# Softmax sums as two float32r parts, formed one step later, in a two-branch attention layer

## The chip, the cores and the metric

The kernel runs on one core of one Trainium2 chip. The metric is the device time of one execution in microseconds, the median of several executions. Engines are named as in the profile: PE (TensorE), DVE (VectorE), ACT (ScalarE), POOL (GpSimd), SP (SyncE, which issues the DMAs here).

## The reference

One encoder layer over 2048 prompt tokens and 512 sample tokens, all in float32. The stage around the change is softmax attention in two branches of 8 heads each (grouped-query, then latent):

```python
s = jnp.einsum('bqgrd,bkgd->bgrqk', qblk, k, preferred_element_type=jnp.float32) * scale
p = jax.nn.softmax(s, axis=-1).astype(v.dtype)
return jnp.einsum('bgrqk,bkgd->bqgrd', p, v)
```

Ahead of it stand the modulated RMS norm, the input projections, norms and rotations of queries and keys; behind it the gated output projections. Neither is touched.

## The kernel before

A number that float32r cannot hold is kept as a high part (its float32r rounding) and a low part (the rest), and products are made from the parts.

**Jobs and steps.** `attention` works through 80 jobs (`specs`): branch, head, and query chunk c of 512 queries. Chunks 0 to 3 are long jobs (2048 keys, 16 key tiles, 8 pairs), chunk 4 is a short one (512 keys, 2 pairs). Keys lie on partitions. One step of the main loop handles one pair n of key tiles; there are 34 steps a head. The order on each engine is the order in which the loop emits (manual schedule).

**One step.** `scores` writes the pair's scores into one of two `st` banks of PSUM (L980: 2 matmuls a key tile in the first branch, 3 in the second). ACT exponentiates the bank twice: rounded to float32r into `ph` (L983, six buffers, the high part), and in place in float32 (L984). `lows` has DVE subtract the two into `pl` (L993, four buffers, the low part), which also frees the bank. Two steps later (`BACK`; three for a job's first pair) `values` multiplies both parts with the values: `pv` (X, one bank, L1003) and `py` (Y, one bank, L1004); at most three key tiles in a step. Between them `advance` issues the maximum stream of a job some 12 steps ahead: two matmuls into the single `mp` bank (L947), reduced by DVE (L950). Since a first pair waits three steps, a step with no value matmuls follows each long job; the prediction calls it the hole. It is the step of pair 2 of the next job.

**Sums.** The softmax sum of a query is row 64 of Y. The low parts bring theirs in through columns of ones in `vt`. For the high parts of a long job, POOL adds the pairs n < `direct` = 7 into `acc` (L986), folds its two halves (L988), and PE adds the fold through the selector `sel` in one float32 matmul (L1008) behind the last key tile. The last pair goes straight in through a float32r selector (L1006). Short jobs use the selector for all their tiles.

**Job end.** `finish` copies X and Y out on ACT (L1015, L1016); POOL adds Y to the lower half of X (L1027) and, three steps later, the two halves (L1029); SP stores sums and output.

Of the kernel before, what the change touches and what calls it, by code (L numbers as in the profile page):

```python
# [9 lines left out]
F32 = mybir.dt.float32  # L10
F32R = mybir.dt.float32r
AF = mybir.ActivationFunctionType
ALU = mybir.AluOpType
# [4 lines left out]
P = 128  # L18
# [5 lines left out]
CH = 512  # L24
# [119 lines left out]
VW = 130  # L144
# [614 lines left out]
def attention(tc, nc, env, h4):  # L759
    e = NS(env)  # L760
    dma, nm, f32 = e.dma, e.nm, e.f32
    ha, fl, filler, cur, rest = h4
    kp = Pool(tc, "kp", "left")
# [25 lines left out]

    zero_q(kp)  # L790
    zero_q(kp)
    sel = [kp.tile([P, VW - 64], t, name=f"sel{n}") for n, t in enumerate((F32, F32R))]
    for a in (sel[0], f32(sel[1])):
        nc.vector.memset(a, 0.0)
        nc.vector.memset(a[:, 64:VW - 64], 1.0)
    tops = [[kp.tile([P, 32], F32, name=f"m{s}{n}") for s in "pt"] for n in range(3)]
    for m, _ in tops:
        nc.vector.memset(m, 0.0)
# [44 lines left out]
    def start(i, br, h, c):  # L843

        j = Job()
        j.br, j.h, j.c = br, h, c
        j.last = (br, h, c) == specs[-1]
        smp = int(c == 4)
        j.nk = (NS_TOK if smp else NP_TOK) // P
        j.direct = 0 if smp else j.nk // 2 - 1  # L850
        j.k1, j.k2, j.vt = kcur[(*kv_of(br, h), smp)]
        j.k3 = k3s[smp]
        qn, qr = q_src(br, h, c)
        j.qz = qzs[i % 3]
        j.qm = kp.tile([P, CH], F32R, tag="qm", name=nm("qm"), bufs=4)
        if br == 0:
            dma(f32(j.qm), qn[0].partition_broadcast(2))
            j.km = j.k1
            j.scale = SC_A
        else:  # L860
            dma(f32(j.qm[0:64, :]), qn[0])
            dma(f32(j.qm[64:128, :]), qr[0].partition_broadcast(2))
            j.km = j.k2
            j.scale = SC_B
        j.mx = kp.tile([P, 4, 2], F32, tag="mx", name=nm("mx"), bufs=3)
        return j
# [15 lines left out]
    at = Pool(tc, "at", "left")  # L882
# [35 lines left out]
    jobs = []  # L918
# [7 lines left out]
    def due(last=False):  # L926
        while queue and (last or queue[0][0] <= clock[0]):
            queue.pop(0)[2]()
# [37 lines left out]
            later(1, row)  # L966
            yield True

    def scores(j, n):

        if n == 0:
            if j.direct:
                j.acc = at.tile([P, 2, CH], F32, tag="acc", name=nm("acc"), bufs=2)
            j.hs, j.ls = [], []
        st = pp.tile([P, 2, CH], F32, tag="st", name=nm("st"), bufs=2)
        for a in range(2):
            kt = 2 * n + a
            ps = j.passes(j, slice(kt * P, (kt + 1) * P))
            for i, (k, q) in enumerate(ps):
                nc.tensor.matmul(st[:, a, :], lhsT=k, rhs=q, start=(i == 0), stop=(i == len(ps) - 1))  # L980
        h = at.tile([P, 2, CH], F32R, tag="ph", name=nm("ph"), bufs=6)
        j.hs.append(h)
        nc.scalar.activation(out=h, in_=st, func=AF.Exp, scale=j.scale)  # L983
        nc.scalar.activation(out=st, in_=st, func=AF.Exp, scale=j.scale)  # L984
        if 0 < n < j.direct:
            nc.gpsimd.tensor_tensor(out=j.acc, in0=f32(j.hs[0]) if n == 1 else j.acc, in1=f32(h), op=ALU.add)  # L986
            if n == j.direct - 1:
                nc.gpsimd.tensor_tensor(out=j.acc[:, 0, :], in0=j.acc[:, 0, :], in1=j.acc[:, 1, :], op=ALU.add)  # L988
        return st

    def lows(j, st):
        l = at.tile([P, 2, CH], F32R, tag="pl", name=nm("pl"), bufs=4)
        nc.vector.tensor_tensor(out=l, in0=st, in1=f32(j.hs[-1]), op=ALU.subtract)  # L993
        j.ls.append(l)

    def values(j, kt):

        if kt == 0:
            j.X, j.Y = x_bank(), y_bank()
        n, a = kt // 2, kt % 2  # L1000
        y = j.Y[0:VW - 64, :]
        st, sp = kt == 0, kt == j.nk - 1
        nc.tensor.matmul(j.X, lhsT=j.vt[:, kt, 0:P], rhs=j.hs[n][:, a, :], start=st, stop=sp)  # L1003
        nc.tensor.matmul(y, lhsT=j.vt[:, kt, 64:VW], rhs=j.ls[n][:, a, :], start=st, stop=False)  # L1004
        if n >= j.direct:
            nc.tensor.matmul(y, lhsT=sel[1], rhs=j.hs[n][:, a, :], start=False, stop=sp and not j.direct)  # L1006
        if sp and j.direct:
            nc.tensor.matmul(y, lhsT=sel[0], rhs=j.acc[:, 0, :], start=False, stop=True)  # L1008
        return j if sp else None

    def finish(j):

        y = at.tile([VW - 64, CH], F32, tag="y", name=nm("ys"), bufs=2)
        xa = at.tile([P, CH], F32, tag="xa", name=nm("xa"), bufs=2)
        nc.scalar.copy(out=xa, in_=j.X)  # L1015
        nc.scalar.copy(out=y, in_=j.Y[0:VW - 64, :])  # L1016
        later(1, lambda: dma(e.sums[j.br][j.c, j.h:j.h + 1, :], y[64:65, :]))
        if j.h == 7 and not j.last:
            for k, step in enumerate(inverse(nc, e, at, j.br, j.c)):
                later(6 + 2 * k, step)  # L1020
        if (j.br, j.h, j.c) == (1, 7, 0):
            for k, step in enumerate(tail_load(nc, e, wt, 1, 0, first_y)):
                later(13 + 3 * k, step)

        def rest():
            s = at.tile([64, CH], F32, tag="s", name=nm("s"), bufs=2)
            nc.gpsimd.tensor_tensor(out=xa[0:64, :], in0=xa[0:64, :], in1=y[0:64, :], op=ALU.add)  # L1027
            later(1, lambda: dma(s, xa[64:128, :]))
            later(3, lambda: nc.gpsimd.tensor_tensor(out=s, in0=s, in1=xa[0:64, :], op=ALU.add))  # L1029
            later(5, lambda: dma(  # L1030
                e.o_s[j.br][j.h // 2, 64 * (j.h % 2):64 * (j.h % 2) + 64, j.c * CH:(j.c + 1) * CH], s))

        return rest
# [4 lines left out]
    def advance(to):  # L1038
        while done[0] < to and next(stream, None) is not None:
            done[0] += 1  # L1040
# [5 lines left out]
    with contextlib.ExitStack() as order:  # L1046
# [14 lines left out]
        passes = {0: start_main(0, *specs[0])}  # L1061
        order.close()
        order.enter_context(tc.manual_schedule(engines={eng.PE, eng.Activation, eng.DVE, eng.Pool, eng.SP}))
        ready, g = [], -1
        while g + 1 < len(steps) or ready:
            g += 1
            clock[0] = g
            st, rest = None, None
            if g < len(steps):
                i, n = steps[g]  # L1070
                br, h, c = specs[i]
                if c < 2 and n == 4:
                    late = [0]

                    def post_later(out, in_):
                        later(late[0], lambda: post_now(out, in_))
                        late[0] += 1

                    if c == 0 and i + 5 < len(specs):
                        load_k(*kv_of(*specs[i + 5][0:2]), 0, post_later)  # L1080
                    if c == 1:
                        load_k(*kv_of(br, h), 1, post_later)
                if n == 0:
                    for k in range(i + 1, min(i + 3, len(specs))):
                        if k not in passes and (k == i + 1 or pairs[i + 1] < 8):
                            passes[k] = start_main(k, *specs[k])
                    jobs[i].passes = passes.pop(i)
                    if specs[i] == (1, 0, 0):
                        for k in range(4):
                            later(24 * k + 4, lambda k=k: wa.append(load_raw(nc, e, wt, e.a_out, k)))  # L1090
                            later(24 * k + 12, lambda k=k: wa.append(
                                split_raw(nc, e, wt, "wa", wa.pop(), k, nc.gpsimd)))
                        for m, step in enumerate(tail_load(nc, e, wt, 0, 0, first_y)):
                            later(24 * m + 100, step)
                        later(180, lambda: y0.extend(split_y(nc, e, wt, 0, first_y.pop())))
                st = scores(jobs[i], n)
                ready += [(g + BACK + (n == 0), jobs[i], 2 * n + a) for a in range(2)]
            now = sum(r[0] <= g for r in ready)
            for m in range(min(now, 3)):
                if m == 1:  # L1100
                    advance(lead + g + 1)
                _, j, kt = ready.pop(0)
                if values(j, kt):
                    rest = finish(j)
            if now < 2:
                advance(lead + g + 1)
            due()
            if st is not None:
                lows(jobs[i], st)
            if rest:  # L1110
                rest()
# [217 lines left out]
```

## Time and profile before

| | |
|---|---|
| median of 3 runs | 3220.47 us (3214.39 to 3221.25) |
| profiled execution | 3216.27 us, span 3214.5 us |
| granted TensorE clock | 0.994 of full speed (2.4 GHz) |
| busy share of the span | PE 98%, DVE 60%, POOL 57%, ACT 51% |
| attention, first branch | about 1233 to 1928 us |
| attention, second branch | about 1928 to 2746 us |

How to read it: a matmul record begins when its rows start to flow and ends some way into the next one's, so records overlap, and a busy PE says little by itself. The distance of two starts tells what a matmul costs. A record that is longer than its like, or starts later, has been held.

### The profile page before, as it was taken

The numbers are of one execution on the slowest core, as the hardware profiler recorded it, in microseconds if no ns is written. First come the engines' busy times: TensorE is split into PE (matmuls) and PEld (weight loads), VectorE is DVE, ScalarE is ACT, GpSimd is POOL, SyncE is SP. The second block draws the span as 40 slices with busy tenths as digits, with TensorE's granted clock in tenths as the row PEclk, the third lists the DMA queues.
The fourth block names the chain that finished last, engine by engine and source line by source line (L and its number), as shares of the span: only waits on it lengthen the run. The fifth ranks groups of instructions, "written<-read, shape, count | busy, mean of one in ns | idle before, by whom it ended". The sixth has DMA issues, their size and how long they took to land.

```text
span 3214.5 us, 41877 instructions
## 1 busy us (share of the span) xinstructions
PE 3146.4 (98%) x15214; PEld 2538.8 (79%) x15214; DVE 1919.8 (60%) x2441; ACT 1635.3 (51%) x2169; POOL 1820.4 (57%) x1124
## 2 busy tenths in 40 slices
PE   7999999999999989999999999999999999899999
PEld 6988889988889877777777777777777777799997
DVE  5733214532205227999999998887887887544443
ACT  5332234232224226888888877777676777321122
POOL 6422123421224336888888887777776778644443
PEclk9999999999999999999999999999999999999999
DMA  8445542365634741112111134433433222665552
GB/s 244 146 150 204 189 159 90 120 201 180 205 103 151 223 144 55 40 37 68 42 48 36 38 88 105 99 91 84 94 93 86 67 66 69 197 190 164 162 175 73
DMA packets 283922, 383.89 MB, mean 119 GB/s; under 512 B 31916, under 2 KB 185844, under 8 KB 281252
## 3 DMA queue, kind: packets, MB, share of 16 engines
q1 hardware_dynamic: 283716, 381.22, 40.1%
q8 instruction: 120, 1.97, 0.3%
q14 instruction: 86, 0.70, 0.1%
HBM read 251.52 MB, written 118.96 MB: 115 GB/s over the span
## 4 chain that ended last, share of the span: by engine, by line
PE 87%; DMA 4%; DVE 3%; issue 2%; ACT 2%; POOL 1%; SPq 1%; ACTq 0%; POOLq 0%; DVEq 0%
PE st L980 18%; PE mm L604 17%; PE mm L340 8%; PE mp L947 8%; PE py L1004 7%; PE pv L1003 7%; PE z L1270 6%; PE ab L1204 6%; PE mm L692 3%; PE py L1008 2%; PE py L1006 1%; SPq L44 1%; PE pv L604 1%; DMA raw<-in_w_in 1%; PE py L604 1%
## 5 line engine op out<-in xcount | busy, mean ns | idle before, releaser
L986 POOL TENSOR_TENSOR acc<-acc,ph 128x1024 f32<-128x1024 f32 x320 | 768.8, 2403 | 56.1 <-ACT ph L983 42.0
L950 DVE TENSOR_REDUCE mx<-mp 128x1 f32<-128x1024 f32 x512 | 625.9, 1222 | 218.1 <-PE mp L947 217.1
L983 ACT ACTIVATE ph<-st 128x1024 fp32r<-128x1024 f32 x544 | 558.5, 1027 | 364.7 <-PE st L980 357.0
L993 DVE TENSOR_TENSOR pl<-st,ph 128x1024 fp32r<-128x1024 f32 x544 | 658.2, 1210 | 37.9 <-ACT st L984 37.5
L984 ACT ACTIVATE st<-st 128x1024 f32<-128x1024 f32 x544 | 555.5, 1021 | 0.0
L209 POOL TENSOR_TENSOR wl<-wraw,wh 128x1536 fp32r<-128x1536 f32 (+3 forms) x59 | 189.0, 3214 | 508.8 <-ACT wh L208 508.2
L980 PE MATMUL st<-qm,k 128*128 128x512 f32 x1024 | 434.1, 424 | 9.1 <-DVE pl L993 8.4
L980 PE MATMUL st<-qz,k 128*128 128x512 f32 x1056 | 416.1, 394 | 0.0
L1003 PE MATMUL pv<-ph,vt 128*128 128x512 f32 x1024 | 404.3, 395 | 4.0 <-ACT xa L1015 3.6
L1004 PE MATMUL py<-pl,vt 128*66 128x512 f32 x1024 | 404.7, 395 | 0.0
L947 PE MATMUL mp<-k,qm 128*128 128x512 f32 x1024 | 323.4, 397 | 0.4 <-DVE mx L950 0.4
L604 PE MATMUL mm<-hh,wh 128*128 128x512 f32 x768 | 302.2, 394 | 0.0
L604 PE MATMUL mm<-hl,wh 128*128 128x512 f32 x768 | 301.8, 393 | 0.0
L604 PE MATMUL mm<-hh,wl 128*128 128x512 f32 x768 | 301.8, 393 | 0.0
L980 PEld LDWEIGHTS st<-qm,k 128*128 128x128 f32 x1024 | 192.2, 188 | 110.2 <-DVE pl L993 35.8
L947 PEld LDWEIGHTS mp<-k,qm 128*128 128x128 f32 x1024 | 190.6, 188 | 73.4 <-DVE mx L950 11.9
L986 POOL TENSOR_TENSOR acc<-ph,ph 128x1024 f32<-128x1024 f32 x64 | 153.0, 2390 | 161.7 <-ACT ph L983 161.7
L1003 PEld LDWEIGHTS pv<-ph,vt 128*128 128x128 f32 x1024 | 192.6, 188 | 61.8 <-ACT xa L1015 10.6
L980 PEld LDWEIGHTS st<-qz,k 128*128 128x128 f32 x1056 | 198.5, 188 | 47.6 <-issue 7.4
L340 PE MATMUL mm<-wh,hh 128*128 128x384 f32 (+1 forms) x640 | 210.9, 330 | 5.1 <-ACT hh L60 2.7
L340 PE MATMUL mm<-wl,hh 128*128 128x384 f32 (+1 forms) x640 | 210.1, 329 | 0.0
L340 PE MATMUL mm<-wh,hl 128*128 128x384 f32 (+1 forms) x640 | 205.8, 330 | 0.0
(235 smaller groups left out, 5782.5 us busy)
## 6 DMA issues: line engine op xcount, KB each, us to landing
wraw<-in_w_in SPq DMA_DIRECT2D x46, 768.0 KB
x<-in_x_prompt SPq DMA_DIRECT2D x32, 512.0 KB
wada<-in_ada_w SPq DMA_DIRECT2D x24, 512.0 KB
raw<-in_w_in SPq DMA_DIRECT2D x48, 256.0 KB
vb<-uv SPq DMA_DIRECT2D x20, 512.0 KB
qm<-aqh SPq DMA_DIRECT2D x40, 256.0 KB
s<-xa SPq DMA_DIRECT2D x80, 128.0 KB
mt<-ma SPq DMA_DIRECT2D x40, 256.0 KB
```

The costliest lines, as they stand in the source:

```text
L340: nc.tensor.matmul(ps[:, 0:n], lhsT=lt, rhs=rt, start=(i == 0), stop=(i == 23))
L604: nc.tensor.matmul(ps, lhsT=lt, rhs=rt[:, k, :], start=(i == 0), stop=(i == 23))
L947: nc.tensor.matmul(mp[:, a, :], lhsT=j.qm[:, qt * P:(qt + 1) * P], rhs=j.km[:, kc * CH:(kc + 1) * CH], start=True, stop=True)
L950: nc.vector.tensor_reduce(out=j.mx[:, n // 2, n % 2:n % 2 + 1], in_=mp.rearrange("p a k -> p (a k)"), axis=AX.X, op=ALU.max)
L980: nc.tensor.matmul(st[:, a, :], lhsT=k, rhs=q, start=(i == 0), stop=(i == len(ps) - 1))
L983: nc.scalar.activation(out=h, in_=st, func=AF.Exp, scale=j.scale)
L984: nc.scalar.activation(out=st, in_=st, func=AF.Exp, scale=j.scale)
L986: nc.gpsimd.tensor_tensor(out=j.acc, in0=f32(j.hs[0]) if n == 1 else j.acc, in1=f32(h), op=ALU.add)
L993: nc.vector.tensor_tensor(out=l, in0=st, in1=f32(j.hs[-1]), op=ALU.subtract)
L1003: nc.tensor.matmul(j.X, lhsT=j.vt[:, kt, 0:P], rhs=j.hs[n][:, a, :], start=st, stop=sp)
L1004: nc.tensor.matmul(y, lhsT=j.vt[:, kt, 64:VW], rhs=j.ls[n][:, a, :], start=st, stop=False)
L1204: nc.tensor.matmul(ps[:, dd, :], lhsT=a, rhs=b, start=(i == 0), stop=(i == 11))
```

## The change

The float32 sum matmul goes. ACT rounds the fold to float32r and POOL subtracts to get its low part (`sum_parts`, one `ph` buffer for both); this is emitted in the next job's first step, between the two exps. Two float32r matmuls (`sums`) add the parts to Y one step after the job's last key tile, which is the hole. The X copy stays where it was (`finish`); the Y copy and all that follows it move one step back (`finish_sums`). In the first branch `direct` is 6: one pair fewer in POOL's sum, two more selector matmuls. There too, the last pair's full exp goes to SBUF (a `pl` buffer) and its low part is subtracted by POOL and not by DVE (`low_by_pool`). Short jobs are as before.

```diff
--- before.py
+++ after.py
@@ -789,10 +789,9 @@
 
     zero_q(kp)
     zero_q(kp)
-    sel = [kp.tile([P, VW - 64], t, name=f"sel{n}") for n, t in enumerate((F32, F32R))]
-    for a in (sel[0], f32(sel[1])):
-        nc.vector.memset(a, 0.0)
-        nc.vector.memset(a[:, 64:VW - 64], 1.0)
+    sel = kp.tile([P, VW - 64], F32R, name="sel")
+    nc.vector.memset(f32(sel), 0.0)
+    nc.vector.memset(f32(sel[:, 64:VW - 64]), 1.0)
     tops = [[kp.tile([P, 32], F32, name=f"m{s}{n}") for s in "pt"] for n in range(3)]
     for m, _ in tops:
         nc.vector.memset(m, 0.0)
@@ -847,7 +846,8 @@
         j.last = (br, h, c) == specs[-1]
         smp = int(c == 4)
         j.nk = (NS_TOK if smp else NP_TOK) // P
-        j.direct = 0 if smp else j.nk // 2 - 1
+        j.parts = not smp
+        j.direct = 0 if smp else j.nk // 2 - 2 + br
         j.k1, j.k2, j.vt = kcur[(*kv_of(br, h), smp)]
         j.k3 = k3s[smp]
         qn, qr = q_src(br, h, c)
@@ -966,7 +966,7 @@
             later(1, row)
             yield True
 
-    def scores(j, n):
+    def scores(j, n, ended):
 
         if n == 0:
             if j.direct:
@@ -981,6 +981,12 @@
         h = at.tile([P, 2, CH], F32R, tag="ph", name=nm("ph"), bufs=6)
         j.hs.append(h)
         nc.scalar.activation(out=h, in_=st, func=AF.Exp, scale=j.scale)
+        if ended:
+            sum_parts(ended)
+        if low_by_pool(j, n):
+            full = at.tile([P, 2, CH], F32, tag="pl", name=nm("pf"), bufs=4)
+            nc.scalar.activation(out=full, in_=st, func=AF.Exp, scale=j.scale)
+            return full
         nc.scalar.activation(out=st, in_=st, func=AF.Exp, scale=j.scale)
         if 0 < n < j.direct:
             nc.gpsimd.tensor_tensor(out=j.acc, in0=f32(j.hs[0]) if n == 1 else j.acc, in1=f32(h), op=ALU.add)
@@ -988,7 +994,22 @@
                 nc.gpsimd.tensor_tensor(out=j.acc[:, 0, :], in0=j.acc[:, 0, :], in1=j.acc[:, 1, :], op=ALU.add)
         return st
 
+    def sum_parts(j):
+
+        a = j.acc[:, 0, :]
+        j.sum = at.tile([P, 2, CH], F32R, tag="ph", name=nm("hl"), bufs=6)
+        nc.scalar.copy(out=j.sum[:, 0, :], in_=a)
+        nc.gpsimd.tensor_tensor(out=j.sum[:, 1, :], in0=a, in1=f32(j.sum[:, 0, :]), op=ALU.subtract)
+
+    def low_by_pool(j, n):
+        return j.br == 0 and j.parts and n == j.nk // 2 - 1
+
     def lows(j, st):
+        if low_by_pool(j, len(j.ls)):
+            l = at.tile([P, 2, CH], F32R, tag="pl", name=nm("pl"), bufs=4)
+            nc.gpsimd.tensor_tensor(out=l, in0=st, in1=f32(j.hs[-1]), op=ALU.subtract)
+            j.ls.append(l)
+            return
         l = at.tile([P, 2, CH], F32R, tag="pl", name=nm("pl"), bufs=4)
         nc.vector.tensor_tensor(out=l, in0=st, in1=f32(j.hs[-1]), op=ALU.subtract)
         j.ls.append(l)
@@ -1003,16 +1024,22 @@
         nc.tensor.matmul(j.X, lhsT=j.vt[:, kt, 0:P], rhs=j.hs[n][:, a, :], start=st, stop=sp)
         nc.tensor.matmul(y, lhsT=j.vt[:, kt, 64:VW], rhs=j.ls[n][:, a, :], start=st, stop=False)
         if n >= j.direct:
-            nc.tensor.matmul(y, lhsT=sel[1], rhs=j.hs[n][:, a, :], start=False, stop=sp and not j.direct)
-        if sp and j.direct:
-            nc.tensor.matmul(y, lhsT=sel[0], rhs=j.acc[:, 0, :], start=False, stop=True)
+            nc.tensor.matmul(y, lhsT=sel, rhs=j.hs[n][:, a, :], start=False, stop=sp and not j.direct)
         return j if sp else None
 
+    def sums(j):
+        for k in range(2):
+            nc.tensor.matmul(j.Y[0:VW - 64, :], lhsT=sel, rhs=j.sum[:, k, :], start=False, stop=k == 1)
+
     def finish(j):
 
+        j.xa = at.tile([P, CH], F32, tag="xa", name=nm("xa"), bufs=2)
+        nc.scalar.copy(out=j.xa, in_=j.X)
+
+    def finish_sums(j):
+
+        xa = j.xa
         y = at.tile([VW - 64, CH], F32, tag="y", name=nm("ys"), bufs=2)
-        xa = at.tile([P, CH], F32, tag="xa", name=nm("xa"), bufs=2)
-        nc.scalar.copy(out=xa, in_=j.X)
         nc.scalar.copy(out=y, in_=j.Y[0:VW - 64, :])
         later(1, lambda: dma(e.sums[j.br][j.c, j.h:j.h + 1, :], y[64:65, :]))
         if j.h == 7 and not j.last:
@@ -1061,8 +1088,8 @@
         passes = {0: start_main(0, *specs[0])}
         order.close()
         order.enter_context(tc.manual_schedule(engines={eng.PE, eng.Activation, eng.DVE, eng.Pool, eng.SP}))
-        ready, g = [], -1
-        while g + 1 < len(steps) or ready:
+        ready, ending, g = [], [], -1
+        while g + 1 < len(steps) or ready or ending:
             g += 1
             clock[0] = g
             st, rest = None, None
@@ -1093,7 +1120,7 @@
                         for m, step in enumerate(tail_load(nc, e, wt, 0, 0, first_y)):
                             later(24 * m + 100, step)
                         later(180, lambda: y0.extend(split_y(nc, e, wt, 0, first_y.pop())))
-                st = scores(jobs[i], n)
+                st = scores(jobs[i], n, jobs[i - 1] if i and n == 0 and jobs[i - 1].parts else None)
                 ready += [(g + BACK + (n == 0), jobs[i], 2 * n + a) for a in range(2)]
             now = sum(r[0] <= g for r in ready)
             for m in range(min(now, 3)):
@@ -1101,9 +1128,17 @@
                     advance(lead + g + 1)
                 _, j, kt = ready.pop(0)
                 if values(j, kt):
-                    rest = finish(j)
+                    finish(j)
+                    if j.parts:
+                        ending.append((g + 1, j))
+                    else:
+                        rest = finish_sums(j)
             if now < 2:
                 advance(lead + g + 1)
+            if ending and ending[0][0] == g:
+                j = ending.pop(0)[1]
+                sums(j)
+                rest = finish_sums(j)
             due()
             if st is not None:
                 lows(jobs[i], st)
```

PE at the end of a first-branch long job and after. Ahead of these rows stands the last key tile's `pv`. Before:

```order
L1004 MATMUL py_10908<-pl_11012,vt_9397 66x512
L1006 MATMUL py_10908<-ph_10997,sel_9418 66x512
L1008 MATMUL py_10908<-acc_10834,sel_9417 66x512
L980 MATMUL st_11062<-qm_10636,k_9395 128x512
L980 MATMUL st_11062<-qz_10194,k_9396 128x512
L980 MATMUL st_11062<-qm_10636,k_9395 128x512
L980 MATMUL st_11062<-qz_10194,k_9396 128x512
L947 MATMUL mp_11074<-k_9395,qm_10822 128x512 x2
```

Now, from the hole's maximum matmuls to the next job's first matmul into Y (`py_11099`; `hl` holds the sum's two parts):

```order
L947 MATMUL mp_11077<-k_9395,qm_10819 128x512 x2
L1032 MATMUL py_10909<-hl_11026,sel 66x512 x2
L980 MATMUL st_11089<-qm_10633,k_9395 128x512
L980 MATMUL st_11089<-qz_10191,k_9396 128x512
L980 MATMUL st_11089<-qm_10633,k_9395 128x512
L980 MATMUL st_11089<-qz_10191,k_9396 128x512
L1024 MATMUL pv_11098<-ph_11024,vt_9397 128x512
L1025 MATMUL py_11099<-pl_11040,vt_9397 66x512
```

The sum's matmul stood ahead of the hole's four score matmuls; its two parts now stand behind them, with the next step's four score matmuls and one value matmul between them and the first one that writes the next job's Y.

ACT at the same place, from the first exp of the next job's pair 0 on. Before:

```order
L983 ACTIVATE ph_11021<-st_11016 128x1024
L984 ACTIVATE st_11016<-st_11016 128x1024
L983 ACTIVATE ph_11039<-st_11034 128x1024
L984 ACTIVATE st_11034<-st_11034 128x1024
L1015 COPY xa_11055<-pv_10907 128x512
L1016 COPY ys_11054<-py_10908 66x512
L983 ACTIVATE ph_11067<-st_11062 128x1024
L984 ACTIVATE st_11062<-st_11062 128x1024
L983 ACTIVATE ph_11087<-st_11082 128x1024
```

Now:

```order
L983 ACTIVATE ph_11024<-st_11019 128x1024
L1001 CAST hl_11026<-acc_10831 128x512
L990 ACTIVATE st_11019<-st_11019 128x1024
L983 ACTIVATE ph_11047<-st_11042 128x1024
L990 ACTIVATE st_11042<-st_11042 128x1024
L1037 COPY xa_11061<-pv_10908 128x512
L983 ACTIVATE ph_11070<-st_11065 128x1024
L990 ACTIVATE st_11065<-st_11065 128x1024
L1043 COPY ys_11083<-py_10909 66x512
L983 ACTIVATE ph_11094<-st_11089 128x1024
L990 ACTIVATE st_11089<-st_11089 128x1024
```

The copy of Y (`ys`) stood ahead of the hole's two exps, right behind that of X, and stands behind them now; between the two exps of pair 0 stands the rounding of the sum (`CAST hl`).

POOL in the first branch, from the job's last additions to the next job's first. Before:

```order
L1029 TENSOR_TENSOR s_10879<-s_10879,xa_10874 64x512
L986 TENSOR_TENSOR acc_10834<-acc_10834,ph_10955 128x1024
L986 TENSOR_TENSOR acc_10834<-acc_10834,ph_10975 128x1024
L988 TENSOR_TENSOR acc_10834<-acc_10834 128x512
L986 TENSOR_TENSOR acc_11015<-ph_11021,ph_11039 128x1024
```

Now:

```order
L992 TENSOR_TENSOR acc_10831<-acc_10831,ph_10931 128x1024
L992 TENSOR_TENSOR acc_10831<-acc_10831,ph_10957 128x1024
L994 TENSOR_TENSOR acc_10831<-acc_10831 128x512
L1056 TENSOR_TENSOR s_10897<-s_10897,xa_10874 64x512
L1010 TENSOR_TENSOR pl_11015<-pf_11000,ph_10998 128x1024
L1002 TENSOR_TENSOR hl_11026<-acc_10831,hl_11026 128x512
L992 TENSOR_TENSOR acc_11018<-ph_11024,ph_11047 128x1024
L992 TENSOR_TENSOR acc_11018<-acc_11018,ph_11070 128x1024
```

One addition is gone; the addition of the previous job's halves (`s`) moved behind the fold, and the last pair's low part (`pl`) and the sum's low part (`hl`) stand between it and the next job's first addition.

## Rows read from the trace of the kernel before

**Rows 1.** Windows of the two branches: busy us (instructions) by engine, then clock, DMA.

```profile
1233.00:1928.00 695.00, 688.39 (x2850) 492.05 (x2849) 640.39 (x615) 560.83 (x616) 592.65 (x299) 1.00 0.19 49
1928.00:2746.00 818.00, 810.24 (x3413) 603.74 (x3412) 646.31 (x613) 573.30 (x634) 621.08 (x313) 1.00 0.35 85
```

**Rows 2.** Timeline, PE, end of a first-branch job: start, us, engine, line, tiles.

```profile
1709.14 1.02 PE L1008 MATMUL py<-acc,sel 128*66 128x512 f32 x2
...
1710.24 0.39 PE L980 MATMUL st<-qz,k 128*128 128x512 f32 x1
...
1712.56 0.39 PE L1004 MATMUL py<-pl,vt 128*66 128x512 f32 x1
1712.87 0.74 PE L947 MATMUL mp<-k,qm 128*128 128x512 f32 x2
1713.44 0.39 PE L1003 MATMUL pv<-ph,vt 128*128 128x512 f32 x1
...
1714.13 0.40 PE L1004 MATMUL py<-pl,vt 128*66 128x512 f32 x1
1714.44 0.50 PE L980 MATMUL st<-qm,k 128*128 128x512 f32 x1
1714.78 0.39 PE L980 MATMUL st<-qz,k 128*128 128x512 f32 x1
```

**Rows 3.** Timeline, PE: f32 sums one head later, and a head apart.

```profile
1796.71 1.02 PE L1008 MATMUL py<-acc,sel 128*66 128x512 f32 x2
...
2082.35 1.02 PE L1008 MATMUL py<-acc,sel 128*66 128x512 f32 x2
...
2183.57 1.02 PE L1008 MATMUL py<-acc,sel 128*66 128x512 f32 x2
```

**Rows 4.** Timeline, PE, first branch: first and last held maximum matmul of 23.

```profile
1253.70 0.73 PE L947 MATMUL mp<-k,qm 128*128 128x512 f32 x2
...
1910.23 0.73 PE L947 MATMUL mp<-k,qm 128*128 128x512 f32 x2
```

**Rows 5.** Timeline, PE, behind a short job: last score matmul, first value matmuls.

```profile
1758.61 0.40 PE L980 MATMUL st<-qz,k 128*128 128x512 f32 x1
1759.51 0.50 PE L1003 MATMUL pv<-ph,vt 128*128 128x512 f32 x1 [0.51 <-ACT xa L1015]
...
1760.27 0.62 PE L947 MATMUL mp<-k,qm 128*128 128x512 f32 x2
```

**Rows 6.** Timeline, ACT, same place: last exp, copies of X and Y.

```profile
1757.93 1.02 ACT L984 ACTIVATE st<-st 128x1024 f32<-128x1024 f32 x1
1758.88 0.59 ACT L1015 COPY xa<-pv 128x512 f32<-128x512 f32 x1
1759.35 0.58 ACT L1016 COPY ys<-py 66x512 f32<-66x512 f32 x1
```

**Rows 7.** Timeline, ACT, the two exps of the hole of rows 2.

```profile
1711.19 1.02 ACT L983 ACTIVATE ph<-st 128x1024 fp32r<-128x1024 f32 x1 [0.41 <-PE st L980]
1712.11 1.02 ACT L984 ACTIVATE st<-st 128x1024 f32<-128x1024 f32 x1
```

**Rows 8.** Timeline, ACT, second branch: first exp of a hole.

```profile
2186.05 1.03 ACT L983 ACTIVATE ph<-st 128x1024 fp32r<-128x1024 f32 x1 [0.85 <-PE st L980]
```

**Rows 9.** Groups of instructions by line: count, busy us, mean ns, idle before.

```profile
L986 POOL TENSOR_TENSOR acc<-acc,ph 128x1024 f32<-128x1024 f32 x320 | 768.8, 2403 | 56.1 <-ACT ph L983 42.0 <-DMA s<-xa 0.5 <-DMA qz<-mt 0.2
...
L993 DVE TENSOR_TENSOR pl<-st,ph 128x1024 fp32r<-128x1024 f32 x544 | 658.2, 1210 | 37.9 <-ACT st L984 37.5
...
L984 ACT ACTIVATE st<-st 128x1024 f32<-128x1024 f32 x544 | 555.5, 1021 | 0.0
...
L988 POOL TENSOR_TENSOR acc<-acc 128x512 f32<-128x512 f32 x64 | 82.7, 1292 | 5.0
...
L258 POOL TENSOR_TENSOR ada<-wada,ada 128x1024 fp32r<-128x1024 f32 x8 | 27.5, 3446 | 7.4 <-ACT ada L256 7.4
...
L1147 POOL TENSOR_TENSOR wal<-raw,wah 128x1024 fp32r<-128x1024 f32 x4 | 9.6, 2402 | 3.8 <-ACT wah L1146 3.8
```

## The prediction

> **What bounds the kernel now.** I read the windows of the two branches first [rows 1]: the granted clock is 1.00 and PE is busy 688 of 695 us in the first branch and 810 of 818 us in the second. That busy figure is not yet proof, because matmul records overlap, so I then counted issue slots in the timeline. Ten 512-column matmuls issue between 1710.24 and 1712.56 us [rows 2], 0.232 us each; I use 0.231 us as one slot. A head of five jobs takes 1796.71 - 1709.14 = 87.6 us in the first branch and 2183.57 - 2082.35 = 101.2 us in the second [rows 2, 3]. Its slots: in the first branch a long job issues 32 score, 32 value, 16 maximum and 2 selector matmuls, 82 slots, and one f32 sum; the short job issues 24. The f32 sum starts at 1709.14; the second score matmul behind it starts at 1710.24, so the first began at 1710.01, and the sum held PE for 0.87 us [rows 2]. Together 352 x 0.231 + 4 x 0.87 = 84.8 us of 87.6. The second branch has two more score matmuls for each key tile: 420 x 0.231 + 4 x 0.87 = 100.5 of 101.2. So PE's order sets the end in both branches, and what counts is slots and PE's waits, 2.8 us a head in the first branch and 0.7 in the second.
>
> Where the 2.8 us lie: after the hole (the step in which no value matmuls are due) PE is held four times, 1712.87 - 1712.56 - 0.23 = 0.08, then 0.11, 0.08 and 0.11 us, 0.38 us together [rows 2]. The same piece stands 23 times in the branch, the first at 1253.70 and the last at 1910.23 [rows 4]. Those are waits for DVE (the single maximum bank, the score banks). Once a head, behind the short job, the next job's first value matmuls wait for ACT's copies of X and Y: 1759.51 - 1758.61 - 0.23 = 0.67 us and then 1760.27 - 1759.51 - 0.46 = 0.30, 0.97 in all [rows 5]. The rest, 2.8 - 0.97 - 3 x 0.38 = 0.7 us a head, is scattered.
>
> **The price of a copy just ahead of its reader.** Rows 5 and 6 give it for this kernel: the Y copy starts 0.95 + 0.47 us after the exp before it; the matmul into Y issues at 1760.27 - 0.23 = 1760.04, so 0.69 us after its copy's start at 1759.35. The copies themselves start 0.95 us after the start of the exp ahead of them (1758.88 - 1757.93).
>
> **Slots.** The f32 sum (0.87 us) becomes two slots (0.46). In the second branch that is all: -0.41 us x 32 long jobs = -13.1 us. In the first, two more selector matmuls are added: 4 x 0.231 - 0.87 = +0.05, x 32 = +1.7 us.
>
> **The Y copy, one step later.** It used to follow the X copy ahead of the hole; now the sum is formed in the hole and Y is copied behind the hole's two exps, while the next step's second value matmul already wants the single Y bank. First branch, T being the hole's first score matmul: the first exp starts at T + 1.18 (1710.01 to 1711.19), the second 0.92 later, the copy 0.95 after that, T + 3.05, and Y is free for PE at T + 3.05 + 0.69 = 3.74 [rows 2, 5, 6, 7]. PE gets there after 8 slots of the hole and 5 of the next step, 13 x 0.231 = 3.00. A wait of 0.74 us in each long job, 32 x 0.74 = +23.7 us. Second branch: the exp starts 1.61 us after the hole's first score matmul (2183.57 + 0.87 = 2184.44 to 2186.05 [rows 3, 8]), Y is free at 1.61 + 0.92 + 0.95 + 0.69 = 4.17, PE arrives after 17 slots at 3.93: 0.24 x 32 = +7.7 us. Ends: 0 and these values, if something else already holds PE there; I take the full values, as the chain starts from PE's own score matmuls and slides with them.
>
> **Waits that go.** The 0.38 us behind the hole are waits for DVE at the matmuls right behind the held one; PE now arrives there 0.74 us later, and DVE has one subtraction less a job (1.21 us [rows 9]). I let all 23 go: -8.7 us. The short job's 0.97 us stays (its end is not changed), and the scattered 0.7 us a head stays, with 0 as its other end.
>
> **The low part on GpSimd.** Its duration is not there for this pair of tiles. Nearest: the additions of the same size in the same stage, 2.40 us, and the same subtraction at the weights, 2.40; far end: the same subtraction at the modulation, 3.45 [rows 9]. I take 2.40, the stage's own row. With T7 the last pair's first score matmul, the full exp ends near T7 + 1.18 + 0.92 + 1.02 = 3.1 and the low part at 5.5; its matmul stands 27 slots behind T7, at 6.24. So 0.7 us of cover if GpSimd is free, and its work of a long job, 6 x 2.40 + 4 x 1.29 = 19.6 us, fits into the job's 20.8. Cost taken as 0; if that cover is gone, each microsecond more is PE's.
>
> In the 3.45 us row VectorE ran the other half of the same subtraction, both inputs in SBUF. The Trainium skill (SBUF — State Buffer, section "SBUF: two separate sides") says that such a VectorE instruction and a GpSimd instruction shut each other out of a shared port pair for whole instructions. By that rule the 2.40 stands here, since VectorE's subtraction in attention reads one input from PSUM; the trace agrees, 320 additions beside it with a mean of 2403 ns [rows 9].
>
> **Hidden parts.** ACT's copy of the sum's high part delays the second exp of pair 0 by about 0.47 us, the distance of two copies; its bank is wanted 24 slots (5.5 us) after its score matmuls, exp and subtraction done, DVE frees it near 1.18 + 0.92 + 0.47 + 1.02 + 1.21 = 4.8 [rows 6, 7, 9]. The sum's low part on GpSimd (1.29) is wanted 30 slots (6.9 us) after pair 0's first score matmul, and can be there at about 5. The fold that ACT's copy reads lies a pair earlier in the first branch; in the second GpSimd has 19.6 us of work for 23 us. The rows of sums, the half s and the stores leave SP a step later; behind them stand loads for a later job. One selector tile and its fills less: nothing.
>
> **Sum.** First branch 1.7 + 23.7 - 8.7 = +16.7, second -13.1 + 7.7 = -5.4, together +11.3 us on the profiled execution's 3216.27: **3227.6 us**. That execution lies 4.2 us under the runs' median of 3220.47, inside their spread of 6.9 us. A measurement tells about 0.2% (6.4 us) from no change.
>
> **Rivals.**
> *The scattered DVE waits go too* (chance 0.20). DVE loses 32 x 1.21 = 39 us of work in the first branch; 8 x 0.7 = 5.6 us of PE's waits could go with it: 3222. Against: the subtraction removed is the last pair's, and the waits come from the work before it as well.
> *Y's copy does not hold PE* (0.10): faster. The mechanism is the hole itself: two slots of filling take the place of the f32 sum, and PE is never early at Y. It decides at a copy that starts by T + 2.31 in the first branch and T + 3.24 in the second, against 3.05 and 3.48. Then 1.7 - 8.7 - 13.1 = -20.1: 3196. For it speaks that before the change no long job's Y copy held PE; against it that the copy now stands behind both exps in ACT's order, and the short job's end shows the very wait.
> *GpSimd becomes the bound of the first branch* (0.10). At 3.45 us the low part ends at T7 + 6.6, 0.4 behind its matmul even if GpSimd starts at once, and its job of 20.6 us has no room: 0.4 to 1.0 us x 32, about 20 us more, 3248.
>
> **Chances.** The forecast has 0.60. Its own error of some 5 us puts 0.05 of that under +6.4 us: slower by over 0.2% 0.55 + 0.10 = 0.65. The scattered waits put 0.18 within 0.2%, 0.23 with that 0.05, and 0.02, where more goes than counted, beyond it: faster 0.10 + 0.02 = 0.12. The range reaches to the GpSimd case on one side, 3247; on the other beyond the scattered waits (3222) to a Y wait that costs half, 3227.6 - 15.7 = 3212, with 4 us for the runs' spread: 3208.
>
> **What would show it.** Right: before the matmul into Y, PE idle released by ACT's Y copy in nearly every long job; jobs of the first branch about 0.5 us longer, of the second about 0.2 shorter; maximum matmuls behind the hole without their held 0.74 us records; the low part on GpSimd at 2.4 us and no PE wait for it. Wrong: Y's matmul issuing with no gap (then faster), PE or DVE waiting for GpSimd (then slower still), or exps waiting for the tile rings.

## The result, and the profile after

| | before | after |
|---|---|---|
| median | 3219.05 us (4 runs, 3214.39 to 3221.25) | 3234.93 us (4 runs, 3232.00 to 3241.51) |
| profiled execution | 3216.27 us, span 3214.5 | 3236.64 us, span 3234.8 |
| first branch, from its score matmul at some 1230 us to the second branch's first on `q` (its second score matmul) | 1227.41 to 1928.14: 700.7 us | 1231.71 to 1944.07: 712.4 us |
| second branch, to the start of the last Y copy | to 2746.43: 818.3 us | to 2769.61: 825.5 us |

The ratio is 1.0054, 95% interval 1.0042 to 1.0066: 15.9 us slower, well clear of noise. The two profiled executions differ by 20.4 us. Of that 11.7 lie in the first branch and 7.2 in the second; another 4.3 us were there before attention began, in code that the change does not touch, and 2.8 came back behind it. Over the profiled executions of this study the first of these marks lay anywhere from 1226.2 to 1234.4 us, so I count neither.

The windows of the two branches after the change, as in [rows 1]:

```profile
1233.00:1928.00 695.00, 680.65 (x2855) 489.02 (x2856) 600.74 (x572) 564.63 (x637) 621.76 (x325) 1.00 0.19 48
1928.00:2746.00 818.00, 807.96 (x3418) 602.64 (x3417) 659.23 (x620) 587.30 (x666) 657.84 (x344) 1.00 0.34 84
```

PE is busy 7.7 us less of the first window than before and DVE 40 us less, while GpSimd gained 29: PE stands idle more, and no other engine is full (GpSimd, the next, 621.76 of 695 us). Where it stands shows the timeline of PE at the hole of a first-branch job, against [rows 2]:

```profile
1791.74 0.40 PE L980 MATMUL st<-qm,k 128*128 128x512 f32 x1
...
1792.68 0.63 PE L947 MATMUL mp<-k,qm 128*128 128x512 f32 x2
1793.14 0.63 PE L1032 MATMUL py<-hl,sel 128*66 128x512 f32 x2
1793.65 0.50 PE L980 MATMUL st<-qm,k 128*128 128x512 f32 x1
1793.98 0.39 PE L980 MATMUL st<-qz,k 128*128 128x512 f32 x1
...
1794.67 0.40 PE L1024 MATMUL pv<-ph,vt 128*128 128x512 f32 x1
1795.38 0.45 PE L1025 MATMUL py<-pl,vt 128*66 128x512 f32 x1 [0.31 <-ACT ys L1043]
1795.66 0.63 PE L947 MATMUL mp<-k,qm 128*128 128x512 f32 x2
```

The hole's first score matmul is at 1791.74. The sums follow the maximum matmuls at 1793.14. The next step's first value matmul goes at 1794.67; the matmul into Y should follow 0.23 us later and comes at 1795.66 - 0.23 = 1795.43. It is released by the Y copy, and ACT shows why, in the same place:

```profile
1792.88 1.03 ACT L983 ACTIVATE ph<-st 128x1024 fp32r<-128x1024 f32 x1 [0.27 <-PE st L980]
1793.80 1.02 ACT L990 ACTIVATE st<-st 128x1024 f32<-128x1024 f32 x1
1794.74 0.58 ACT L1043 COPY ys<-py 66x512 f32<-66x512 f32 x1
```

First exp, second exp, copy: the copy starts 3.00 us after 1791.74 (forecast 3.05) and PE gets Y 0.69 us behind its start, at 3.69 (forecast 3.74). So PE is 0.69 us late there; some 0.15 of them fall on the score matmul at 1793.65, held by DVE, and 0.5 on Y. The maximum matmuls behind it take 0.46 us to the next matmul, not the 0.57 of [rows 2]. All instructions of the Y copy's line, and who waited for them:

```profile
L1043 ACT COPY ys<-py x80: 578/583/591, 1257.7 to 2769.6; 66x512 f32<-66x512 f32 x80
...
  PEld py L1025: 42.5, 79
  PE py L1025: 9.6, 33
```

In the kernel before, weight loads waited for the Y copy in 16 places, all behind short jobs:

```profile
  PEld py L1004: 5.4, 16
```

### The profile page after: what moved, and what is told of

The parts are those of the page before. It is cut to its first block, busy times and chain, and to the rows that moved or that the text cites. A ratio compares the mean times of both kernels' runs of the same rounds, so it can differ in the third digit from the quotient of the medians.

```text
span 3234.8 us, 42209 instructions
## 1 busy us (share of the span) xinstructions
PE 3152.3 (97%) x15278; PEld 2545.6 (79%) x15278; DVE 1888.9 (58%) x2407; ACT 1662.6 (51%) x2233; POOL 1903.6 (59%) x1188
## 4 chain that ended last, share of the span: by engine, by line
PE 80%; DMA 5%; ACT 4%; issue 3%; POOL 3%; DVE 3%; SPq 1%; ACTq 0%; POOLq 0%; DVEq 0%
PE mm L604 17%; PE st L980 16%; PE mm L340 8%; PE py L1025 7%; PE pv L1024 7%; PE mp L947 6%; PE z L1305 6%; PE ab L1239 6%; PE mm L692 3%; ACT st L990 2%; PE py L1027 2%; SPq L44 1%; POOL acc L992 1%; PE pv L604 1%; DMA raw<-in_w_in 1%
## 5 line engine op out<-in xcount | busy, mean ns | idle before, releaser
L992 POOL TENSOR_TENSOR acc<-acc,ph 128x1024 f32<-128x1024 f32 x288 | 691.6, 2401 | 76.2 <-ACT ph L983 68.3
L1014 DVE TENSOR_TENSOR pl<-st,ph 128x1024 fp32r<-128x1024 f32 x512 | 620.9, 1213 | 57.9 <-ACT st L990 55.4
L990 ACT ACTIVATE st<-st 128x1024 f32<-128x1024 f32 x512 | 522.1, 1020 | 0.0
L980 PE MATMUL st<-qm,k 128*128 128x512 f32 x1024 | 410.7, 401 | 9.4 <-DVE pl L1014 8.6
L442 ACT ACTIVATE gt<-mm 128x512 f32<-128x512 f32 x96 | 57.2, 597 | 285.3 <-PE mm L604 233.5
```

## The experiments

Each kernel was timed in five rounds beside the kernel before. The times of the two branches are from the profiled execution of each, from the marks of the table above.

| kernel | median, us | ratio, 95% interval | first, second branch, us |
|---|---|---|---|
| before | 3217.8 to 3219.1 | 1 | 700.7, 818.3 |
| changed | 3234.9 | 1.0054 (1.0042 to 1.0066) | 712.4, 825.5 |
| 1 sums in the last step | 3214.6 | 0.9991 (0.9982 to 1.0000) | 703.4, 815.3 |
| 2 Y copy between the exps | 3218.0 | 1.0001 (0.9993 to 1.0010) | 702.4, 819.6 |
| 3 first branch alone | 3228.9 | 1.0037 (1.0024 to 1.0050) | 711.7, 819.2 |
| 4 second branch alone | 3221.5 | 1.0018 (1.0009 to 1.0027) | 699.9, 823.5 |
| 5 second, in step, splits on DVE | 3215.2 | 0.9991 (0.9982 to 1.0000) | 700.4, 818.7 |
| 6 no pair fewer | 3304.9 | 1.0268 (1.0254 to 1.0282) | 779.7, 825.2 |
| 7 low part by DVE | 3236.6 | 1.0057 (1.0044 to 1.0069) | 714.0, 825.3 |
| 8 f32 sum in the hole | 3217.3 | 0.9999 (0.9991 to 1.0008) | 699.3, 819.7 |
| 9 as 5, splits on GpSimd | 3211.5 | 0.9980 (0.9971 to 0.9989) | 702.1, 811.5 |
| 10 rounding after the exp | 3230.2 | 1.0037 (1.0025 to 1.0050) | 712.4, 821.6 |
| 11 9 and 10 together | 3208.5 | 0.9970 (0.9959 to 0.9982) | 701.0, 807.1 |

**1. The sums back in the last key tile's step.**

```diff
                 if values(j, kt):
                     finish(j)
                     if j.parts:
-                        ending.append((g + 1, j))
-                    else:
-                        rest = finish_sums(j)
+                        sums(j)
+                    rest = finish_sums(j)
```

> The changed kernel with the two sum matmuls put back into the step of the job's last key tile, and the Y copy behind the X copy as before. Theory A (PE waits for the late Y copy: 20.4 us in the first branch and 9.0 in the second by the changed kernel's trace): those 29 us go, some 9 us of waits for VectorE behind the hole come back in the first branch, so about 3215 us, 0.2% under the kernel before. Theory B (the time is GpSimd's: the sum's low part and the last pair's low part come late): the sums now wait for the sum's low part, no gain, 3235 us or more, and PE idle released by GpSimd.

3214.6 us, 20 less than the change, as theory A had it. The waits of matmuls into Y, by releaser:

```profile
  ACT hl L1001: 5.5, 2
  ACT ys L1043: 4.5, 16
  POOL hl L1002: 3.6, 4
```

What is left for the Y copy are the 16 places behind short jobs. GpSimd's part of the sum is late in two places only and ACT's in one, at the end of attention (matmul and weight load are counted apart).

**2. The Y copy ahead of the second exp.** The second exp of the hole is emitted behind the copy:

```diff
+        return st if hold else second(j, n, st)
+
+    def second(j, n, st):
+        h = j.hs[-1]
         if low_by_pool(j, n):
...
                 sums(j)
                 rest = finish_sums(j)
+                if st is not None:
+                    st = second(jobs[i], n, st)
```

> The changed kernel with the sums in the hole as they are, but the Y copy put ahead of the hole's second exp on ScalarE. Theory A: the copy starts 0.7 us earlier than in the changed kernel in the first branch and 0.7 in the second, PE's wait before the first matmul into Y falls from 0.63 and 0.28 us a job to about 0, so about 3206 us, up to 3214 if VectorE takes part of it back. Theory B: GpSimd's work is as it was, 3230 us or more.

```profile
  PEld py L1029: 4.4, 16
```

The waits for Y are gone here too, and 17 us with them, with nothing on GpSimd changed. It stayed 4 us above the expected range: the second branch kept 819.6 us, which this kernel was not made to explain; experiment 10 shows a part of the reason in the changed kernel.

**3 and 4. One branch alone** (`j.parts` true in one branch only, the f32 sum and its selector kept for the other).

> The change in the first branch alone; the second branch is as in the kernel before. The prediction's terms give +16.7 us, about 3236 us; the profiled pair gives 11.6 us between the starts of the two branches, about 3231 us. If GpSimd is the cause it is all here: the whole 16 us, 3235.

> The change in the second branch alone (no pair fewer, no low part by GpSimd there); the first branch is as in the kernel before. The prediction's terms give -5.4 us, about 3214 us; the profiled pair has +7.3 us in this branch, about 3226 us. Theory A with the trace's own waits: -13.1 + 9.0 plus 3.7 at the end of attention, 3219 us.

10.9 and 3.4 us, together 14.3 of the 15.9. The first branch costs what its trace said and less than forecast; the second costs, where the forecast had a gain of 5.4.

**8. The late copy without the parts.** The kernel before, with its f32 matmul moved into the hole (a `sums` with that one matmul) and the Y copy split off as in the change.

> The kernel before with its f32 sum moved into the hole and the Y copy behind the hole's exps; no parts, seven pairs, low parts by VectorE. The same late copy, but the f32 sum fills 0.87 us of the hole: PE gets to the first matmul into Y at 6 x 0.231 + 0.87 + 5 x 0.231 = 3.41 us after the hole's first score matmul in the first branch against 3.74, a wait of 0.33, and at 4.34 against 4.17, none, in the second. With 8.7 us of VectorE waits covered: +2 us, 3218 to 3222. If a late copy costs by itself, whatever fills the hole, +15 us or more.

3217.3 us: no difference. Weight loads do wait for Y in the first branch, where the sum was expected to leave a gap; with the 16 places behind short jobs it is half of what they wait in the changed kernel:

```profile
  PEld py L1004: 22.9, 48
```

These waits are made up for, as expected, by waits for DVE that go: those before maximum matmuls fall from 11.9 us in the kernel before to 1.2. So in net the step's delay alone costs nothing measurable. It costs together with the cheap parts: what they save in the hole, PE spends waiting at the next matmul into Y.

**6. The pair put back into GpSimd's sum.** `j.direct = j.nk // 2 - 1` in both branches.

> The changed kernel with the pair put back into GpSimd's sum in the first branch (direct 7): two selector matmuls less on PE (-14.8 us), one addition of 2.40 us more on GpSimd. GpSimd's work of a long job is then 22.0 us against a job of 20.7: if GpSimd has no room in the change as made, each of the 32 long jobs grows by 1.3 us and the idle it cannot avoid, +40 to +70 us on 3235, PE waiting for the low part. If GpSimd has room, 3220 us.

```profile
L1010 POOL TENSOR_TENSOR pl<-pf,ph x32: 2342/2356/2392, 1247.1 to 2003.4; 128x1024 fp32r<-128x1024 f32 x32
...
  PEld py L1025: 74.2, 32
  PE py L1025: 60.3, 32
```

The upper end: 70 us, 2.2 us for each of 32 jobs. The low part takes 2.36 us, but GpSimd starts it late every time; PE waits between these two, which stand 0.23 us apart otherwise:

```profile
1539.49 0.39 PE L1024 MATMUL pv<-ph,vt 128*128 128x512 f32 x1
1542.45 0.45 PE L1025 MATMUL py<-pl,vt 128*66 128x512 f32 x1 [2.58 <-POOL pl L1010]
```

So the pair fewer is what the low part by GpSimd requires; the third rival was one addition away.

**7. The low part by DVE again** (`low_by_pool` returns False).

> The changed kernel with the last pair's low part made by VectorE in the first branch as in the second (direct stays 6). If VectorE's waits were already covered by PE's wait for the Y copy, and GpSimd's low part is in time, the move brings nothing and costs nothing: 3233 to 3237 us. If the relief of VectorE counts, 32 x 1.2 us of it at most: up to 3270. If GpSimd's low part is a cost, below 3230.

```profile
  PEld py L1025: 44.2, 79
  PE py L1025: 11.4, 33
```

3236.6 against 3234.9 us, within both spreads, and the waits for the Y copy are nearly the same (42.5 and 9.6 us in the changed kernel). The move to GpSimd neither cost nor gained anything measurable, and so taking 1.2 us a job off DVE was not worth anything measurable either.

**10. The rounding behind the second exp.** In the second branch of the changed kernel two things stood out that the forecast did not have. ACT, then PE at the same two places:

```profile
2071.44 1.03 ACT L983 ACTIVATE ph<-st 128x1024 fp32r<-128x1024 f32 x1 [0.84 <-PE st L980]
2074.62 0.62 ACT L1001 CAST hl<-acc 128x512 fp32r<-128x512 f32 x1 [2.15 <-POOL acc L994]
2075.15 1.01 ACT L990 ACTIVATE st<-st 128x1024 f32<-128x1024 f32 x1
...
2760.84 0.62 ACT L1001 CAST hl<-acc 128x512 fp32r<-128x512 f32 x1 [5.29 <-POOL acc L994]
```

```profile
2077.47 0.50 PE L980 MATMUL st<-qm,k 128*128 128x512 f32 x1 [1.49 <-DVE pl L1014]
...
2761.51 0.53 PE L1032 MATMUL py<-hl,sel 128*66 128x512 f32 x1 [3.01 <-ACT hl L1001]
```

The rounding of the sum waits 2.15 us for GpSimd's fold, which comes late because GpSimd has worked almost without a gap since it split one of the output weights (at 2057.49 us); the second exp stands behind it, DVE's subtraction behind that, and PE finds the score bank taken for 1.49 us. At the end of attention, where GpSimd also prepares the output stage, the same wait is 5.29 us and PE stands 3.01 us, before the sum's matmul itself. In all:

```profile
L1001 ACT CAST hl<-acc x64: 605/610/621, 1251.3 to 2760.8; 128x512 fp32r<-128x512 f32 x64
...
  POOL acc L994: 10.3, 5
```

```diff
         nc.scalar.activation(out=h, in_=st, func=AF.Exp, scale=j.scale)
-        if ended:
-            sum_parts(ended)
...
         nc.scalar.activation(out=st, in_=st, func=AF.Exp, scale=j.scale)
+        if ended:
+            sum_parts(ended)
```

> The changed kernel with ScalarE's rounding of the sum put behind the second exp of pair 0 instead of between the two exps, in both branches. If the loss in the second branch comes from that rounding waiting for GpSimd's fold (10.3 us of ScalarE idle in 5 places) with an exp behind it, the PE waits of 0.46, 1.65, 0.48 and 0.45 us at the hole's first score matmul go, and the end of attention loses part of its 6 us: 3228 to 3232 us, and the wait for the Y copy stays as it is. If the rounding is no cause, 3235.

3230.2 us, 4.8 less than the change. The intervals of the two ratios still overlap a little, so the size is uncertain; the profiles put 3.9 us of it into the second branch (825.5 to 821.6) and nothing into the first. The same place, and the line's waits:

```profile
2067.89 1.03 ACT L983 ACTIVATE ph<-st 128x1024 fp32r<-128x1024 f32 x1 [0.84 <-PE st L980]
2068.81 1.02 ACT L988 ACTIVATE st<-st 128x1024 f32<-128x1024 f32 x1
2071.07 0.62 ACT L1001 CAST hl<-acc 128x512 fp32r<-128x512 f32 x1 [1.24 <-POOL acc L994]
```

```profile
L1001 ACT CAST hl<-acc x64: 600/607/622, 1249.2 to 2754.4; 128x512 fp32r<-128x512 f32 x64
...
  POOL acc L994: 5.6, 2
```

ACT still waits for the fold, but with the exp done, and DVE has its input. The hole's first score matmul no longer waits. What the move does not take away is the wait at the end of attention, where the sum's matmul itself wants the fold; the kernel before waited there too, for a shorter time. This run, then the kernel before:

```profile
2755.04 0.48 PE L1032 MATMUL py<-hl,sel 128*66 128x512 f32 x1 [2.99 <-ACT hl L1001]
...
2741.81 1.07 PE L1008 MATMUL py<-acc,sel 128*66 128x512 f32 x2 [1.51 <-POOL acc L988]
```

**5, 9 and 11. Towards a faster kernel.** 5: parts in the second branch only, sums in the last step, the last long job (1, 7, 3) with its f32 sum, the weights' low parts (`split_raw` of "wa") on DVE. 9: the same with those on GpSimd. 11: 9 with the edit of 10.

> Towards a version that beats the kernel before: the two parts in the second branch alone, with the sum matmuls in the step of the last key tile; the last long job keeps its f32 sum, and the low parts of the four output weights split inside the second branch are made by VectorE instead of GpSimd. Theory A with its late addition (in the second branch ScalarE's rounding of the sum waits for GpSimd where GpSimd has other work, and holds the exps behind it): the first branch as before, the second -13.1 us with at most 3 us of waits left, 3205 to 3210 us. If the second branch loses its gain to something else (the extra rounding on ScalarE in every job, say), 3214 or more, as in the run with the sums in the step of the last key tile.

> As the run of the second branch with the sums in the step of the last key tile and an f32 sum in the last long job, but the output weights' low parts are made by GpSimd again, as in the kernel before. In that run PE stood 1.46, 2.44, 2.41 and 1.04 us at the four places of these splits, waiting for VectorE's subtraction, 7.4 us in all. If VectorE's queue behind a split was the cause, some 5 to 7 us come back, 3207 to 3211 us, and the four waits are gone or under 1 us each. If the second branch loses its gain to something that both runs share, 3215.

> The first kernel of this call with the rounding behind the second exp of pair 0. The sums, in the step of the last key tile, want the low part 28 slots (6.5 us) after pair 0's first score matmul; behind the exp it can be there about 1.65 + 0.92 + 0.95 + 0.6 + 1.3 = 5.5 us after it. If the rounding holds an exp at the weights' splits only: 1 to 3 us less than without the move, 3205 to 3210. If the low part is late now, PE waits at the sums in every long job and it is slower than without.

5 missed its 3205 to 3210. The cure was the fault: DVE, then PE, at one of the four splits:

```profile
2039.01 1.99 DVE L1185 TENSOR_TENSOR wal<-raw,wah 128x1024 fp32r<-128x1024 f32 x1 [1.57 <-ACT wah L1184]
2040.92 1.21 DVE L1016 TENSOR_TENSOR pl<-st,ph 128x1024 fp32r<-128x1024 f32 x1
```

```profile
2039.52 0.39 PE L1027 MATMUL py<-pl,vt 128*66 128x512 f32 x1
2042.19 0.51 PE L982 MATMUL st<-qm,k 128*128 128x512 f32 x1 [2.28 <-DVE pl L1016]
```

The split holds DVE for 1.99 us just when a score bank waits to be freed, and PE stands 2.28 us. The shortest of the four took 1.23. GpSimd in the same place:

```profile
2038.62 1.30 POOL L1060 TENSOR_TENSOR s<-s,xa 64x512 f32<-64x512 f32 x1
2039.87 2.25 POOL L1058 TENSOR_TENSOR xa<-xa,ys 64x512 f32<-64x512 f32 x1
```

GpSimd's first addition runs until 2039.92. If the split worked only from about then, its 1.2 us end at 2041.1 (measured 2041.00), and the second addition, 1.29 us by its group in the changed kernel, would end 1.29 us behind that, at 2042.29 (measured 2042.12). So each seems to have stood for the other in turn. That is what the Trainium skill says (SBUF — State Buffer, section "SBUF: two separate sides") of a VectorE instruction with two inputs in SBUF, as this split has, beside one of GpSimd; these three rows agree with it to 0.2 us, and the other splits fit: two that began during an addition of GpSimd took 1.65 and 1.72 us, and the one of 1.23 us began with GpSimd idle. No run isolates it. DVE's subtraction in attention reads one input from PSUM and keeps its 1.21 us. Back on GpSimd the four waits fell to one of 1.4 us, and 9 came to 3211.5, half a microsecond above its range. 11 came to 3208.5 us, ratio 0.9970 (0.9959 to 0.9982): 9 us under the kernel before, with the second branch at 807.1 us, 11.2 less than before; the slots alone were to give 0.41 us in each of its 31 jobs with parts, 12.7.

## Why the prediction was right, and where it was not

The forecast of 3227.6 us had the sign, the mechanism and the range (3208 to 3247); the time came 7.3 us above it, 15.9 us over before against the sum's 11.3. The total is nearer than its parts, and that is luck: alone, the first branch cost 10.9 us where 16.7 were forecast, and the second 3.4 where a gain of 5.4 was, so the two errors partly cancel.

- **The f32 sum's price and the slots: right.** With the Y wait and the late rounding taken away, the second branch of experiment 11 gained 11.2 of the 12.7 us that its 31 jobs were to give.
- **The wait for the late Y copy: right in mechanism, a little too large in the first branch.** Copy and reader stand where the rows put them, within 0.05 us. Over the branch the timeline gives 0.67 us at each of 31 holes, 20.8 us against 23.7; the last job's hole already holds score matmuls of the second branch. Of each 0.67 some 0.17 stand at the score matmul that DVE holds and 0.5 at Y. In the second branch such gaps sum to 9.2 us against 7.7. Experiments 1 and 2 take the wait away by two different edits and recover 20 and 17 us.
- **The waits for DVE that go: right.** The held maximum matmuls are gone. So are 2.1 us of a single wait at the start of the branch. With 1.7 us for the slots, 20.8 - 8.9 - 2.1 + 1.7 is 11.5 of the 11.7 us measured; the forecast's 16.7 has 23.7 in place of the 20.8 and lacks the 2.1.
- **The scattered waits: stayed, as taken.** Experiment 7 shows no gain from DVE's relief.
- **The low part on GpSimd: right.** Forecast 2.40 us and no wait; measured:

```profile
L1010 POOL TENSOR_TENSOR pl<-pf,ph x32: 2388/2404/2418, 1250.1 to 1939.1; 128x1024 fp32r<-128x1024 f32 x32
...
  PEld py L1025: 1.9, 7
```

- **The failed step: "in the second GpSimd has 19.6 us of work for 23 us"**, by which the rounding of the sum was to find its fold ready. That is the mean job. Five jobs of the second branch carry other work on GpSimd as well, and ACT waited 10.3 us there, with an exp behind it. Experiment 10 gives back 4.8 us. The term of the second branch was to be -5.4 us and measured +3.4 alone (experiment 4), and +7.2 in the profiled pair. Of those 12.6 us the Y wait makes 1.5 and the rounding 3.0 at four holes. The forecast also had nothing for the end of attention, where PE waits 3.01 us for the sum's high part and 0.81 for the low one, against 1.51 before. Some 3 us more are TensorE's clock (an estimate from the distances of starts there, 0.43 us for 0.23). The changed kernel behind two waits of PE, 5.09 us for DVE until 2493.05 and that at the end of attention; then the kernel before at the end:

```profile
2493.00:2498.00 5.00, 4.95 (x12) 3.68 (x13) 2.88 (x5) 1.92 (x2) 0.76 (x1) 0.50 0.00 0
2762.80:2767.80 5.00, 3.70 (x8) 2.16 (x9) 2.32 (x3) 2.42 (x4) 1.28 (x2) 0.50 0.15 30
...
2743.00:2746.00 3.00, 2.56 (x12) 1.63 (x12) 0.00 (x0) 0.55 (x2) 1.28 (x1) 1.00 0.25 50
```

  The granted clock is 0.50 in the first two. In the kernel before it fell too behind the wait for DVE (4.59 us there), for a shorter stretch, and it stayed at 1.00 at the end. What is left, some 3 us, is not assigned; where the branch was not changed it took 818.3 and 819.2 us.
- **The rivals.** That Y does not hold PE falls with the rows above. That GpSimd is the bound falls for the change as made; experiment 6 shows it one addition further.

Not tried: a second Y bank.

## What to carry to other kernels

When a result is produced later, ask who next writes into its buffer: one bank and a copy placed behind other work of an in-order engine turn a saving into a wait at that writer, here 0.41 us saved and some 0.27 waited in a job of the second branch, and in the first, where nothing was saved, 0.67 waited. An instruction that may wait belongs behind the work that others need, not in front of it. And check whether an engine has room in the fullest job, not in the mean one.

## What was not expected of the hardware

In experiment 6 PE waited about 2 us once a job, and the granted clock of its first branch fell. The windows around one such wait (released at 1542.45 us), with the clock ahead of the last two columns:

```profile
1538.00:1542.40 4.40, 1.88 (x9) 1.14 (x7) 1.94 (x2) 2.74 (x4) 4.32 (x4) 1.00 0.87 205
1543.50:1546.50 3.00, 3.00 (x8) 2.15 (x8) 2.35 (x2) 0.59 (x2) 2.46 (x2) 0.50 0.27 82
1547.00:1551.00 4.00, 3.56 (x16) 2.37 (x15) 3.20 (x3) 4.00 (x5) 3.03 (x2) 1.00 0.28 74
```

The clock is 1.00 up to the wait, 0.50 for a stretch right behind it (of the two levels 1.2 and 2.4 GHz the lower), and 1.00 again; the matmuls there issue 0.43 us apart and not 0.23. So a wait of PE can cost more than its own length. The clock fell 11 times in this branch of 32 waits, and its mean there is 0.98; not every such wait was followed by a fall: behind that of 1.58 us released at 1513.04 the clock stayed.
